# A decoder layer's projections: recorded in ticks, with products chained in PSUM, instead of placed by a scheduler

## The chip, the cores and the metric

The kernel runs on one core of one Trainium2 chip. The time is the device time of the whole program in microseconds (us), as the median of three runs. The profile is one further execution of the same program. The engines are named as the profile names them: PE is the matmul engine (PEld its weight loads), DVE the vector engine, ACT the scalar engine, POOL the GpSimd engine, SP the queue from which this kernel issues its DMAs. PSUM is the accumulator memory that PE writes and that ACT and DVE read, in banks of 512 fp32 columns; SBUF is the working memory.

## The reference

One layer of a hybrid decoder on 2048 tokens of width 1024, all in fp32:

```python
nx = rmsnorm(h, attn_norm_g[l])
proj = jnp.einsum('bsd,dp->bsp', nx, w_in[l])          # 1024 -> 3088 columns
gq, gk, gv, gr, glow, dq, dk_, dv_ = jnp.split(proj, split_at, axis=-1)
gate_pre = einsum(glow, gla_gate_w2[l]) + gla_gate_b[l]
glog = jax.nn.log_sigmoid(gate_pre) / GLA_TAU
o_a = gla_mixer(gq, gk, gv, glog)                       # gated linear attention, 4 heads
o_a = rms(o_a) * gla_norm_g[l] * jax.nn.silu(gr)
o_b = dilated_mixer(dq, dk_, dv_, rel_bias)             # windowed attention, 8 heads, 3 dilations
h = h + concat([o_a, o_b]) @ w_out[l]
h = h + square(relu(rmsnorm(h) @ w_ff1)) @ w_ff2
return rmsnorm(h, final_norm_g)
```

The change is in the first lines: the norm, the projection `proj`, the gate and the silu of `gr`. It also moves the factor `gla_norm_g` into the weights `w_out`.

## The kernel before

The program is one function, `emit`, and runs in stages: projections, the two mixers, the output projection, the MLP. An fp32 matmul is made of three fp32r matmuls (`mm3`, lines 136 to 138): a number is split into a high part (ACT copies it to fp32r, "hi") and a low part (DVE subtracts the high part, "lo"), and high by high, low by high and high by low are added up in PSUM.

The projection of 1024 inputs to 3088 columns is done in column groups: `dv` (256 columns twice), `gr` (264 twice, which hold the output gate and the 16 low-rank gate inputs), `gv` (256 twice), called wide here, and `dq`, `dk` (two groups each), `gq` and `gk` (128 twice), called narrow. Each group is computed for 1024 tokens (two blocks of 512) by the Strassen-Winograd scheme: the weights of a group and the tokens are cut into 2 by 2 blocks, and seven products `j` of their sums stand for eight. The token sums, split in hi and lo, stay in SBUF (`TF`, `TB`, tiles `tb`), one pair for each `j`; the second 1024 tokens are normed while the first are multiplied, kept in DRAM (`nTD`), and reloaded (`reload`). The sums of the weight blocks are made on POOL by `prep` (lines 278 to 284, tile `wraw`), which also splits them into `wcomb` (272 to 276).

A narrow product is 12 matmuls of 512 columns into one bank. A wide product is four times (once for each tile of 128 tokens) 12 matmuls of 256 or 264 columns. Each product has a bank of its own, and `product` takes it out at once: `rest` (lines 372 to 389) adds it to the blocks `CX`, `c11` to `c22` in SBUF (tile `acc`). Lines 372, 377 and 385 copy on ACT; 374, 379, 382 and 387 add a bank to a block on DVE; 380, 388 and 389 add block to block on DVE. `finish` then splits or gates the block and stores it; for `gr` it calls, for one tile of 128 tokens at a time, `log_sigmoid`, the multiplications 330 (DVE) and 331 (POOL) and `gate`.

The opening (the first eight token tiles: load, norm, eight transposes on PE, hi and lo) and the first products stand in an order written by hand (`manual_schedule`). From product 5 on the scheduler sets the order of every engine by its own estimate of time. The column groups go `dv, gr, dq, dk, dq, dk, gq, gk, gv`, twice.

The mixers follow. Their head tiles `qs`, `k`, `v`, `nb` are loaded while the last groups are multiplied.

Of the kernel before, what the change touches and what calls it, by code (L numbers as in the profile page):

```python
# [32 lines left out]
XG = (6, 7)  # L33
XSC = {0: (3,), 1: (4,), 2: (5,), 3: (), 4: (6,)}
TOP = (5,)
OTHER = [7, 9, 10, 11, 12, 13] + [14 * k + n for k in (1, 2, 3) for n in (0, 6, 9, 10, 11, 12)]
# [74 lines left out]
def emit(tc, a, stop=99):  # L111
# [37 lines left out]
    V.memset(mhalf, -0.5)  # L149
    xt = const.tile([128, 1024], F32, name="xt")  # L150
# [72 lines left out]
    misc = slot("misc")  # L223
    gB, gnB, w2b = misc[:, :D], misc[:, D:D + 512], misc[:17, D + 512:D + 768]
    gTs = [misc[:17, D + 768 + 128 * i:D + 896 + 128 * i] for i in range(2)]
    GP = 1056
    xp, bp, acc = slot("xp"), slot("bp"), [slot("acc") for _ in range(3)]
    CX, c11, c12, c21, c22, last = [t[:, GP * q:GP * q + GP] for t in acc for q in range(2)]
    C = [[c11, c12], [c21, c22]]
    stg_ring = view(last, (4, 264))  # L230
    xs = [t[:, D * q:D * q + D] for t in (xp, bp) for q in range(2)] + [c21[:, :D], last[:, :D]] * 2
    stg_at = [0]

    def stage():
        stg_at[0] = (stg_at[0] + 1) % 4
        return stg_ring[:, stg_at[0]]

    groups = [("dv", DV, 256), ("gr", GR, 264), ("dq", DQ, 128), ("dk", DK, 128), ("dq", DQ + 256, 128),
              ("dk", DK + 256, 128), ("gq", GQ, 128), ("gk", GK, 128), ("gv", GV, 256)]
    NG = len(groups)  # L240
    scales = {"dq": -0.125, "gq": 0.125}
    order = (1, 2, 5, 6, 3, 4, 7)
    jobs = [(g, j) for g in range(2 * NG) for j in order]
    w_in = a["w_in"].rearrange("o (c p) n -> p (o c) n", p=128)
    raws = [view(slot("wraw"), (2, 4, 264)) for _ in range(2)]
    combs = [slot("wcomb", FR) for _ in range(3)]
    TF = {j: [slot(f"tb{j}", FR) for _ in range(2)] for j in order}
    TB = {j: [view(t, (4, 512)) for t in TF[j]] for j in order}
    nTD = dram.tile([7, 128, 4, 512], F32, name="nTD")

    def load_w(g, n, k):

        if g < 2 * NG:
            _, c0, w = groups[g % NG]
            SP.dma_start(raws[n][:, k, :, :w], w_in[:, 4 * k:4 * k + 4, c0 + n * w:c0 + n * w + w])

    def comb(at, w):

        t = view(combs[at % 3], (2, 4, max(w, 256)))
        return [t[:, q, :, :w] for q in range(2)]  # L260

    def prep(at):

        if at >= len(jobs):
            return
        g, j = jobs[at]
        kind, _, w = groups[g % NG]
        (a11, a12), (a21, a22) = [[raws[n][:, k, :, :w] for k in range(2)] for n in range(2)]
        hi, lo = comb(at, w)
        src = {1: a11, 2: a12, 5: a21, 6: a21, 3: a12, 4: a22, 7: a21}[j]  # L270
        sc = scales.get(kind, 1.0)
        A.activation(hi, src, AF.Copy, scale=sc)  # L272
        if sc == 1.0:
            V.tensor_tensor(lo, src, hi.bitcast(F32), op=OP.subtract)  # L274
        else:
            V.scalar_tensor_tensor(lo, src, sc, hi.bitcast(F32), op0=OP.mult, op1=OP.subtract)
        if j == 2:
            G.tensor_tensor(a21, a21, a22, op=OP.add)  # L278
        if j == 5:
            G.tensor_tensor(a21, a21, a11, op=OP.subtract)  # L280
            load_w(g + 1, 0, 0)
            G.tensor_tensor(a12, a12, a21, op=OP.subtract)
        if j == 6:
            G.tensor_tensor(a21, a22, a21, op=OP.subtract)
        if j == 3:
            load_w(g + 1, 0, 1)
        if j == 4:
            load_w(g + 1, 1, 1)
        if j == 7:
            load_w(g + 1, 1, 0)  # L290

    def gate(glow, t):

        gT = gTs[t % 2]
        V.memset(gT, 1.0)
        pt = ps("d")
        T.transpose(pt[:16, :128], glow, ident)
        V.tensor_copy(gT[:16], pt[:16, :128])
        pg = ps("d")[:, :256]
        T.matmul(pg, gT, w2b, start=True, stop=True)  # L300
        e = stage()[:, :256]
        log_sigmoid(e, pg)
        SP.dma_start(glD[t * 128:t * 128 + 128], e)

    def finish(g, n, k, i):

        kind, c0, w = groups[g % NG]
        tb = 2 * (g // NG) + k
        c = C[n][k]
        if w == 128:  # L310
            tk = slice(512 * tb, 512 * tb + 512)
            if kind in ("gq", "gk"):
                SP.dma_start((gqD if kind == "gq" else gkD)[n, :, tk], c[:, :512])
                return
            pr = (c0 - (DQ if kind == "dq" else DK)) // 128 + n
            hi = c[:, 512:1024].bitcast(FR)
            A.activation(hi, c[:, :512], AF.Copy)
            V.tensor_tensor(c[:, :512], c[:, :512], hi.bitcast(F32), op=OP.subtract)
            SP.dma_start((qD if kind == "dq" else kD)[pr][:, :, tk], view(c, (2, 512)))
            return  # L320
        t = 4 * tb + i
        tk = slice(t * 128, t * 128 + 128)
        s = c[:, i * w:i * w + w]
        if kind == "gr":
            j = n * w
            m = min(w, 512 - j)
            sg = stage()[:, :m]
            log_sigmoid(sg, s[:, :m])
            A.activation(sg, sg, AF.Exp)
            V.tensor_tensor(s[:, :m], sg, s[:, :m], op=OP.mult)  # L330
            G.tensor_tensor(s[:, :m], s[:, :m], gnB[:, j:j + m], op=OP.mult)
            SP.dma_start(srD[tk, j:j + m], s[:, :m])
            if m < w:
                gate(s[:, m:w], t)
            return
        j = n * w
        if kind == "dv":
            SP.dma_start(token_rows(vN[:, j:], t, 512, w), s)
        if i == 3:
            SP.dma_start((vD if kind == "dv" else gvD)[512 * tb:512 * tb + 512, j:j + w].rearrange("(i p) n -> p i n", i=4),  # L340
                         c[:, :4 * w].rearrange("p (i n) -> p i n", i=4))

    banks = [0]

    def product(at, i):

        g, j = jobs[at]
        kind, _, w = groups[g % NG]
        p = ps("acao"[banks[0] % 4])
        banks[0] += 1  # L350
        B, W = TB[j], comb(at, w)
        n = w
        if w == 128:
            n = 512
            for c in range(4):
                mm3(p, W[0][:, c], W[1][:, c], B[0][:, c], B[1][:, c], c == 0, c == 3)
        else:
            p = p[:, :w]
            tk = slice(i * 128, i * 128 + 128)
            for c in range(4):  # L360
                mm3(p, B[0][:, c, tk], B[1][:, c, tk], W[0][:, c], W[1][:, c], c == 0, c == 3)
# [62 lines left out]
    def x_src(t):  # L424
        return (*xs[:6], c22[:, :D], c12[:, :D])[t]
# [1183 lines left out]
```

## Time and profile before

| | us |
|---|---|
| median of three runs | 2332.18 (2328.66 to 2334.69) |
| the profiled execution | 2329.67 |
| its span | 2327.9 |
| last matmul of the projections starts | 568.48 |
| first matmul of the mixers starts | 568.60 |

The span runs from the first to the last instruction. The profile's page gives the busy time of each engine; a matmul's record there runs until its result is written, so records of matmuls that follow each other overlap, and the busy time of PE says little about how densely they are issued. That is read from the distance between starts. A group's row reads: line, engine, operation, out<-in, out and in shape, count, then busy time, mean of one in ns, and the engine's idle time before it with what ended it. A stretch's row gives, for each engine, busy us and in brackets the number of instructions, then the granted clock of PE (1.00 is full), the DMA share and GB/s.

### The profile page before, as it was taken

The numbers are of one execution on the slowest core, as the hardware profiler recorded it, in microseconds if no ns is written. First come the engines' busy times: TensorE is split into PE (matmuls) and PEld (weight loads), VectorE is DVE, ScalarE is ACT, GpSimd is POOL, SyncE is SP. The second block draws the span as 40 slices with busy tenths as digits, with TensorE's granted clock in tenths as the row PEclk, the third lists the DMA queues.
The fourth block names the chain that finished last, engine by engine and source line by source line (L and its number), as shares of the span: only waits on it lengthen the run. The fifth ranks groups of instructions, "written<-read, shape, count | busy, mean of one in ns | idle before, by whom it ended". The sixth has DMA issues, their size and how long they took to land.

```text
span 2327.9 us, 35479 instructions
## 1 busy us (share of the span) xinstructions
PE 2256.6 (97%) x12456; PEld 1946.6 (84%) x12456; DVE 1698.2 (73%) x2925; ACT 1192.7 (51%) x2259; POOL 952.6 (41%) x879
## 2 busy tenths in 40 slices
PE   6999999999999997999999998999999999999998
PEld 5977889779999997888888886888888888888886
DVE  6889767866767777345677778877776968858997
ACT  5575435533777775223555556555563433333544
POOL 4343223434566779100023234323244535423665
PEclk9999999999999999999999999999999999999999
DMA  6457753767568675467644447444469564454573
GB/s 159 122 165 234 234 163 105 238 197 229 190 201 252 233 236 189 155 206 251 225 135 143 144 149 224 147 148 142 153 215 305 203 208 152 136 163 141 167 235 109
DMA packets 340369, 430.77 MB, mean 185 GB/s; under 512 B 20772, under 2 KB 270133, under 8 KB 333662
## 3 DMA queue, kind: packets, MB, share of 16 engines
q1 hardware_dynamic: 340046, 428.24, 57.9%
q8 instruction: 98, 1.61, 0.3%
q14 instruction: 81, 0.66, 0.1%
q10 hardware_dynamic: 144, 0.26, 0.0%
HBM read 276.60 MB, written 156.54 MB: 186 GB/s over the span
## 4 chain that ended last, share of the span: by engine, by line
PE 75%; DVE 9%; DMA 7%; issue 4%; ACT 2%; POOL 2%; SPq 0%; POOLq 0%; DVEq 0%; ACTq 0%
PE ps_a L136 9%; PE ps_a L138 9%; PE ps_a L137 9%; PE ps_c L137 6%; PE ps_c L138 6%; PE ps_c L136 6%; PE ps_a L754 4%; PE ps_d L136 3%; PE ps_d L138 3%; PE ps_d L137 3%; PE ps_d L735 3%; PE ps_c L713 2%; PE ps_c L715 2%; PE ps_o L136 2%; PE ps_o L137 2%
## 5 line engine op out<-in xcount | busy, mean ns | idle before, releaser
L1163 ACT ACTIVATE w1comb<-w1raw 128x512 fp32r<-128x512 f32 x224 | 141.4, 632 | 238.9 <-PE ps_a L138 81.8
L1342 ACT ACTIVATE cs<-rs 128x1024 fp32r<-128x1024 f32 x104 | 109.6, 1055 | 225.7 <-PE ps_c L138 137.6
L1168 DVE TENSOR_TENSOR w1comb<-w1raw,w1comb 128x512 fp32r<-128x512 f32 x224 | 176.1, 787 | 27.7 <-ACT w1comb L1163 27.7
L726 ACT ACTIVATE pe<-pe,O 128x256 f32<-128x256 f32 (+1 forms) x384 | 155.9, 454 | 56.7 <-DVE O L725 52.0
L754 PE MATMUL ps_a<-v,pt 128*128 128x65 f32 x1200 | 178.7, 250 | 0.7 <-DVE pt L744 0.7
L754 PEld LDWEIGHTS ps_a<-v,pt 128*128 128x128 f32 x1200 | 174.5, 193 | 2.3 <-DVE pt L744 0.9
L735 PE MATMUL ps_d<-ident,pe 128*128 128x128 f32 x600 | 159.1, 278 | 0.0
L725 DVE CUSTOM_DVE_ANT_0 pe<-ps_c,nb 128x256 f32<-128x256 f32 (+1 forms) x384 | 126.8, 361 | 42.6 <-PE ps_d L735 17.4
L136 PE MATMUL ps_a<-hb,w1comb 128*128 128x512 f32 x384 | 149.6, 390 | 1.8 <-ACT xt L1211 1.8
L137 PE MATMUL ps_a<-hb,w1comb 128*128 128x512 f32 x384 | 149.5, 389 | 0.4 <-DVE w1comb L1168 0.4
L138 PE MATMUL ps_a<-hb,w1comb 128*128 128x512 f32 x384 | 149.4, 389 | 0.0
L164 POOL TENSOR_TENSOR stats<-stats,mhalf 128x1 f32<-128x1 f32 (+1 forms) x64 | 48.8, 764 | 245.6 <-DVE stats L163 245.6
L1384 DVE TENSOR_TENSOR ct<-rt,ct 128x1024 fp32r<-128x1024 f32 x68 | 137.1, 2016 | 14.6 <-ACT ct L1380 14.5
L272 ACT ACTIVATE wcomb<-wraw 128x512 fp32r<-128x512 f32 (+2 forms) x126 | 96.7, 773 | 94.8 <-POOL wraw L278 19.6
L137 PE MATMUL ps_c<-ct,cs 128*128 128x512 f32 x360 | 140.1, 389 | 0.0
L136 PE MATMUL ps_c<-ct,cs 128*128 128x512 f32 x360 | 140.1, 389 | 0.0
L138 PE MATMUL ps_c<-ct,cs 128*128 128x512 f32 x360 | 140.1, 389 | 0.0
L1268 POOL TENSOR_TENSOR acc<-acc 128x256 f32<-128x256 f32 x75 | 69.8, 941 | 160.8 <-DVE acc L1268 149.7
L274 DVE TENSOR_TENSOR wcomb<-wraw,wcomb 128x512 fp32r<-128x512 f32 (+2 forms) x84 | 101.4, 1212 | 38.4 <-ACT wcomb L272 34.6
L1268 POOL TENSOR_TENSOR xt<-acc,acc 128x256 f32<-128x256 f32 x32 | 28.2, 883 | 229.8 <-ACT acc L1230 214.1
L1349 DVE SCALAR_TENSOR_TENSOR cs<-rs,cs 128x1024 fp32r<-128x1024 f32 (+1 forms) x56 | 96.8, 1736 | 30.1 <-ACT cs L1342 29.9
L136 PE MATMUL ps_a<-wcomb,tb 128*128 128x256 f32 (+1 forms) x336 | 98.6, 294 | 10.7 <-ACT acc L385 3.4
(353 smaller groups left out, 7661.8 us busy)
## 6 DMA issues: line engine op xcount, KB each, us to landing
rs<-actD SPq DMA_DIRECT2D x103, 512.0 KB, 4.3
actD<-acc SPq DMA_DIRECT2D x288, 128.0 KB, 2.8
w1raw<-w_ff SPq DMA_DIRECT2D x32, 1024.0 KB, 6.3
rt<-w_ff SPq DMA_DIRECT2D x24, 1024.0 KB, 7.6
k<-kD SPq DMA_DIRECT2D x16, 1024.0 KB, 8.3
rb<-hTD SPq DMA_DIRECT2D x13, 1024.0 KB, 6.4
wraw<-w_in SPq DMA_DIRECT2D x48, 256.0 KB, 3.7
cmb<-boD SPq DMA_DIRECT2D x16, 528.0 KB, 5.9
```

The costliest lines, as they stand in the source:

```text
L136: T.matmul(out, sh, mh, start=first, stop=False, skip_group_check=more)
L137: T.matmul(out, sl, mh, start=False, stop=False, skip_group_check=more)
L138: T.matmul(out, sh, ml, start=False, stop=last, skip_group_check=more)
L274: V.tensor_tensor(lo, src, hi.bitcast(F32), op=OP.subtract)
L725: V.tensor_tensor_reduce(p, s, bias, scale=1.0, scalar=BIG, op0=OP.add, op1=OP.min, accum_out=nm)
L726: A.activation(p, p, AF.Exp, bias=nm, scale=-1.0)
L735: T.transpose(pb[:, i * 128:i * 128 + 128], src, ident)
L754: T.matmul(self.b.opsum[:, n % 4], self.pt[:, i * 128:i * 128 + 128], self.b.v[:, blk, cols], start=first, stop=last)
L1163: A.activation(c[:, 0], v, AF.Copy)
L1168: V.tensor_tensor(c[:, 1], v, c[:, 0].bitcast(F32), op=OP.subtract)
L1342: A.activation(v[:, 0], x, AF.Copy, scale=float(PRODUCTS[ph // 2][2]))
L1384: V.tensor_tensor(v[:, 1], x, v[:, 0].bitcast(F32), op=OP.subtract)
```

## The change

The stage of the projections is written again. All five engines run it in program order, and the order comes from a list of ticks: `on(t, f, ...)` enters a step, and the loop plays the ticks and records, after a tick's other steps, that tick's matmuls. One tick is 12 matmuls of a wide product (one token tile) or half a narrow product; a wide group is 28 ticks, a narrow one 14. The hi of a product stands five to seven ticks ahead of it, the lo three or four, the evictions one to three behind.

- Products are chained in PSUM. `rest` formed Winograd's sums by adding blocks. Now bank U takes P1, then P6, then P7, and bank W takes P5, then P3, by matmuls that go on adding into the same bank (`more`), and the bank is copied out in between. A group's products go 1, 2, 6, 5, 7, 4, 3. Two tiles of a wide product share one bank. Only `gr` keeps a bank for each product and tile.
- The weight sums are others (four, of which two in each narrow group of the first half are on POOL; all the rest on DVE).
- `dv` of the first 1024 tokens is computed plainly, tile by tile, 24 matmuls of 512 columns each (`dv_piece`), while the tiles are loaded, normed and transposed. So the first Strassen group is `gr`, at tick 32, and there are 17 groups.
- `gr` is gated by whole blocks of four tiles (`gated`, `gate`); `gla_norm_g` is multiplied into `w_out` instead.
- The gain row of the first norm is loaded once and spread over the partitions by two matmuls; 14 transposes of the identity precede it.

The core of the diff:

```diff
-            if j == 1:
-                A.activation(ix, q, AF.Copy)
-            elif j == 2:
-                V.tensor_tensor(i11, q, ix, op=OP.add)
-                finish(g, 0, 0, i)
-            elif j == 5:
-                A.activation(i22, q, AF.Copy)
-            elif j == 6:
-                V.tensor_tensor(ix, q, ix, op=OP.add)
-                V.tensor_tensor(c12, X, c22, op=OP.add)
-            elif j == 3:
-                V.tensor_tensor(i12, q, i12, op=OP.add)
...
-                V.tensor_tensor(ix, q, ix, op=OP.add)
-                V.tensor_tensor(c21, c21, X, op=OP.add)
-                V.tensor_tensor(c22, c22, X, op=OP.add)
...
+        name = {1: "U", 6: "U", 7: "U", 5: "W", 3: "W"}.get(j, "Y") if kind != "gr" else "Y"
+        more = kind != "gr" and j in (6, 7, 3)
+        if w == 128:
+            if i == 0 and not more:
+                held[name, g % 2] = bank()
+            p = held[name, g % 2]
+            for c in (2 * i, 2 * i + 1):
+                mm3(p, W[0][:, c], W[1][:, c], B[0][:, c], B[1][:, c], c == 0 and not more, c == 3, more)
...
+        if j == 1:
+            A.activation(d11, U, AF.Copy)
+        elif j == 6:
+            A.activation(d12, U, AF.Copy)
+        elif j == 7 and not part:
+            A.activation(d21, U, AF.Copy)
+        elif j == 7:
+            V.tensor_tensor(d22, W, d21, op=OP.add)
+        elif j != 5:
+            to, p = {2: (d11, Y), 4: (d21, Y), 3: (d12, W)}[j]
+            V.tensor_tensor(to, p, to, op=OP.add)
...
+            h, l = (b - 5, b - 3) if L == 2 or (early and x == 0) else (b - 7, b - 4)
...
+                on(b + 2, evict, at, 0)
+                if j == 7:
+                    on(b + 3, evict, at, 0, 1)
+        if L == 2:
+            Ps = G if g < 7 else V
+            for n, t, X in ((0, -4, Ps), (1, -2, V), (2, 0, Ps), (3, 2, V)):
+                on(B + t, wsum, g, n, X)
+            for n, k, t in ((0, 0, 5), (1, 1, 12), (1, 0, 13), (0, 1, 15)):
+                for step, dt in enumerate((0, 1, 2)):
+                    on(B + t + dt, finish_narrow, g, n, k, step)
...
+            if n < 8:
+                on(4 * t + 1, tile_T, n)
+                on(4 * t + 2, tile_hi, n)
+                on(4 * t + 2, tile_lo, n)
+                on(4 * t + 3, tile_keep, n)
+                on(4 * t + 4, sums_G, n)
...
+            for m in range(4):
+                on(4 * t + m, dv_piece, t, m)
```

Where it moves instructions, at three places. The opening on PE, up to the second tile's first matmuls. Before (L449 are transposes, L136 to L138 the product 1 of `dv` for tile 0):

```order
L449 MATMUL ps_c<-ident,xp 128x128 x4
L449 MATMUL ps_d<-ident,xp 128x128 x4
L136 MATMUL ps_a<-wcomb,tb_119 128x256
L137 MATMUL ps_a<-wcomb,tb_120 128x256
L138 MATMUL ps_a<-wcomb,tb_119 128x256
```

And now (L724 the identity, L727 the gain row, L649 transposes, L132 to L134 the plain `dv`):

```order
L724 MATMUL ps_a<-ident 128x128 x14
L727 MATMUL ps_c<-xt,one 128x512
L727 MATMUL ps_d<-xt,one 128x512
L649 MATMUL ps_c<-ident,xp 128x128 x4
L649 MATMUL ps_a<-ident,xp 128x128 x4
L132 MATMUL ps_d<-tb_126,tb_114 128x512
L133 MATMUL ps_d<-tb_126,tb_115 128x512
L134 MATMUL ps_d<-tb_127,tb_114 128x512
```

The first products now take all the columns of `dv` at once, with the token tile as the stationary operand.

DVE in the back half of a narrow `dq` group, before: evictions (380 to 389), the splits of the weights (274) and of a finished block (318), the second half's token sums (503 to 508):

```order
L380 TENSOR_TENSOR acc<-acc 128x512
L382 TENSOR_TENSOR acc<-ps_a,acc 128x4x16x8
L503 TENSOR_TENSOR xp<-bp 128x512
L274 TENSOR_TENSOR wcomb<-wraw,wcomb 128x4x128
L507 TENSOR_TENSOR xp<-bp,xp 128x512
L508 TENSOR_TENSOR xp<-xp,bp 128x512
L318 TENSOR_TENSOR acc<-acc 128x512
L274 TENSOR_TENSOR wcomb<-wraw,wcomb 128x4x128
L387 TENSOR_TENSOR acc<-ps_a,acc 128x4x16x8
L274 TENSOR_TENSOR wcomb<-wraw,wcomb 128x4x128
L388 TENSOR_TENSOR acc<-acc 128x512
L389 TENSOR_TENSOR acc<-acc 128x512
```

And now, in a `dq` group of the second half (360 and 363 read a bank, 379 splits a finished block, 288 the weights, 295 are weight sums of the next group, 445 is the gate):

```order
L295 TENSOR_TENSOR wraw<-wraw 128x4x128
L360 TENSOR_TENSOR acc<-ps_a,acc 128x4x16x8
L288 TENSOR_TENSOR wcomb<-wraw,wcomb 128x4x128
L363 TENSOR_TENSOR acc<-ps_o,acc 128x4x16x8
L295 TENSOR_TENSOR wraw<-wraw 128x4x128
L379 TENSOR_TENSOR acc<-acc 128x512
L288 TENSOR_TENSOR wcomb<-wraw,wcomb 128x4x128
L445 SCALAR_TENSOR_TENSOR xt<-ps_d,xt 128x512 x2
L363 TENSOR_TENSOR acc<-ps_a,acc 128x4x16x8
```

Of the five evictions here three are left, each out of a bank; in the whole group seven became four. The weight sums came to DVE.

POOL in the narrow groups of the first half, before (278 to 284 are the four weight sums, 331 the gating of `gr`, 164 a norm's root):

```order
L331 TENSOR_TENSOR acc<-acc,misc 128x248 x4
L278 TENSOR_TENSOR wraw<-wraw 128x4x128
L331 TENSOR_TENSOR acc<-acc,misc 128x248
L280 TENSOR_TENSOR wraw<-wraw 128x4x128
L282 TENSOR_TENSOR wraw<-wraw 128x4x128
L284 TENSOR_TENSOR wraw<-wraw 128x4x128
```

And now (163 is the root, and after the last row of these POOL has no weight sums any more):

```order
L295 TENSOR_TENSOR wraw<-wraw 128x4x128 x6
L163 TENSOR_TENSOR stats<-stats,mhalf 128x1 x2
L295 TENSOR_TENSOR wraw<-wraw 128x4x128 x2
L163 TENSOR_TENSOR stats<-stats,mhalf 128x1 x2
L295 TENSOR_TENSOR wraw<-wraw 128x4x128 x2
```

POOL now makes 12 of the 68 weight sums, where it made all 72, and none of the 32 multiplications of line 331.

757 lines of the change are left out of this document (471 added, 286 removed).

## The prediction, made before the changed kernel ran

> **What bounds the kernel now.** First the page: engines, then the span in slices.
>
> ```profile
> PE 2256.6 (97%) x12456; PEld 1946.6 (84%) x12456; DVE 1698.2 (73%) x2925; ACT 1192.7 (51%) x2259; POOL 952.6 (41%) x879
> PE   6999999999999997999999998999999999999998
> DVE  6889767866767777345677778877776968858997
> PEclk9999999999999999999999999999999999999999
> ```
>
> PE is the bound throughout; the change can only remove time in which PE issues nothing. The projections are the first ten slices, with DVE nearly as full as PE. So next the stretches: the opening, the other projections, the mixers, the rest.
>
> ```profile
> 0.00:100.00 100.00, 76.33 (x520) 71.72 (x520) 69.18 (x96) 49.31 (x86) 45.08 (x32) 0.95 0.56 148
> 100.00:568.60 468.60, 452.19 (x2687) 392.81 (x2688) 348.99 (x526) 230.79 (x457) 166.06 (x124) 0.99 0.62 188
> 568.60:933.00 364.40, 350.98 (x3095) 343.28 (x3094) 265.82 (x1054) 253.94 (x709) 255.76 (x369) 0.99 0.68 221
> ```
>
> Of these, the same view of the products alone (tile wcomb), then of the transposes (tile ident):
>
> ```profile
> 0.00:100.00 100.00, 67.12 (x456) 62.53 (x456) 16.82 (x11) 11.49 (x11) 0.95 0.56 148
> 100.00:568.60 468.60, 434.82 (x2568) 380.21 (x2568) 117.94 (x115) 85.16 (x115) 0.99 0.62 188
> ```
>
> ```profile
> 0.00:100.00 100.00, 11.43 (x64) 9.63 (x64) 0.50 (x2) 0.95 0.56 148
> 100.00:568.60 468.60, 13.69 (x80) 8.73 (x80) 0.00 (x0) 0.99 0.62 188
> ```
>
> How long does a product's matmul hold PE? Records overlap, so I take the distance of starts in two dense stretches: in the chain, 37 steps of 512 columns; in the timeline, 43 steps of 256.
>
> ```profile
> 519.83 0.23 PE ps_a L137
> ...
> 528.22 0.23 PE ps_o L138
> ```
>
> ```profile
> 563.32 0.28 PE L137 MATMUL ps_a<-wcomb,tb 128*128 128x256 f32 x1
> ...
> 568.48 0.28 PE L138 MATMUL ps_o<-wcomb,tb 128*128 128x256 f32 x1
> ```
>
> 8.39 / 37 = 0.227 us and 5.16 / 43 = 0.120 us; for 264 columns I scale to 0.124. The groups by line and shape give the counts (three lines each, so three times these):
>
> ```profile
> L136 PE MATMUL ps_a<-tb,wcomb 128*128 128x512 f32 x168 | 66.3, 395 | 0.0
> L136 PE MATMUL ps_c<-tb,wcomb 128*128 128x512 f32 x84 | 34.3, 409 | 1.8 <-ACT wcomb L272 1.8
> L136 PE MATMUL ps_o<-tb,wcomb 128*128 128x512 f32 x84 | 33.2, 395 | 1.3 <-ACT acc L377 1.3
> L136 PE MATMUL ps_a<-wcomb,tb 128*128 128x264 f32 x112 | 32.0, 286 | 1.2 <-DVE acc L374 1.2
> L136 PE MATMUL ps_c<-wcomb,tb 128*128 128x264 f32 x56 | 16.0, 285 | 0.0
> L136 PE MATMUL ps_o<-wcomb,tb 128*128 128x264 f32 x56 | 16.1, 287 | 1.7 <-DVE acc L374 1.7
> L300 PE MATMUL ps_d<-misc 17*128 17x256 f32 x32 | 11.1, 426 | 0.0
> ```
>
> Opening: 456 x 0.120 = 54.7 us of products and 11.4 of transposes in 100 us; 33.9 lost. After 100 us: 1008 x 0.227 = 228.8, 672 x 0.124 = 83.3, the other 2568 - 1680 = 888 x 0.120 = 106.6, transposes 13.7, gate 11.1: 443.5 of 468.6; 25.1 lost. Together 59 us. (Busy time overstates transposes and gate, so the loss is rather more; a few us of it are bias rows and first scores.)
>
> **The opening.** Its durations, and its chain's first links:
>
> ```profile
> 5.43 1.06 ACT L429 ACTIVATE tb<-xp 128x1024 fp32r<-128x1024 f32 x1 [3.44 <-DMA xp<-x]
> 8.25 1.11 PE L449 MATMUL ps_c<-ident,xp 128*128 128x128 f32 x4 [8.25 <-DVE xp L441]
> L416 ACT ACTIVATE tb<-ps_d 128x512 fp32r<-128x512 f32 x8 | 4.7, 586 | 0.0
> L272 ACT ACTIVATE wcomb<-wraw 128x1024 fp32r<-128x1024 f32 x28 | 29.4, 1054 | 31.5 <-PE ps_c L137 5.9 <-PE ps_o L137 5.4 <-PE ps_o L138 5.0
> L495 DVE SCALAR_TENSOR_TENSOR xp<-xp,stats,misc 128x1024 f32<-128x1024 f32 x8 | 10.2, 1280 | 4.7 <-POOL stats L164 4.4
> L417 DVE TENSOR_TENSOR tb<-ps_d,tb x8: 675/678/681, 12.8 to 68.2; 128x512 fp32r<-128x512 f32 x8
> L417 DVE TENSOR_TENSOR tb<-acc,tb x8: 681/1610/1781, 43.5 to 66.6; 128x512 fp32r<-128x512 f32 x8
> 30.00:40.00 10.00, 7.27 (x41) 7.07 (x41) 8.71 (x10) 6.62 (x13) 8.13 (x5) 0.72 0.20 56
> ```
>
> Tile 0 is transposed at about 8.7 us, its first plain matmul comes at 11.7; nothing is won there. Then ACT's order decides: for each of tiles 1 to 3 a square (1.06 and a read of 0.19), a weight split (1.05), two copies hi and two to keep (4 x 0.59), each behind the transposes that wait for DVE's scale (1.28) and PE's piece. Walked through, tile 1 is transposed at 18, tile 2 at 28, tile 3 at 34, and the pieces of tiles 0 to 2 are done at about 39 us. PE has then done 3 x 24 x 0.227 = 16.3 and 4 x 1.43 (11.43 / 8) = 5.7: 17 lost. For tiles 3 to 7 PE has 24 x 0.227 + 1.43 = 6.9 us each. DVE has four reads of PSUM (0.68), the scale, a root (0.15) and two splits of SBUF tiles (0.68 alone, 1.61 beside POOL): 5.5 to 7.4. So up to 0.5 a tile is lost, 2 us; and 3 for the slow clock seen in the row 30 to 40 (0.72), which a broken-up opening will meet again. Loss 22 us; the ends are 16 (no clock loss, DVE within PE) and 30 (near the 33.9 of before, which has the same chain with less ACT work).
>
> The Trainium skill, "SBUF — State Buffer", § "SBUF: two separate sides", says that DVE and POOL share a port pair as an exclusive lock, so that a DVE operation with two SBUF inputs waits out a whole POOL operation that reads SBUF. The rows of L417 agree (0.68 out of PSUM, up to 1.78 between SBUF tiles). By that rule both POOL sums of a tile could hold DVE up in full and a tile would take 8 to 9 us, the loss 28; by the median row it is 22.
>
> **Added PE work.** `dv` of the first half: 8 x 24 x 0.227 = 43.6 instead of 7 x 4 x 12 x 0.120 = 40.3, so +3.3. The identity and gain matmuls lie ahead of 8.7 us, where PE has nothing else: nothing. The gates' and all other matmuls are the same in number.
>
> **From tick 32 on.** A narrow group is 84 x 0.227 = 19.1 us of PE, a wide one 336 x 0.120 = 40.3 (`gr` 41.7). Against that:
>
> ```profile
> L274 DVE TENSOR_TENSOR wcomb<-wraw,wcomb 128x1024 fp32r<-128x1024 f32 x28 | 44.3, 1583 | 17.3 <-ACT wcomb L272 13.7 <-DMA wraw<-w_in 3.6
> L276 DVE SCALAR_TENSOR_TENSOR wcomb<-wraw,wcomb 128x512 fp32r<-128x512 f32 x42 | 33.3, 799 | 14.0 <-ACT wcomb L272 13.9
> L318 DVE TENSOR_TENSOR acc<-acc 128x512 f32<-128x512 f32 x32 | 31.2, 989 | 0.7 <-ACT acc L317 0.5
> L374 DVE TENSOR_TENSOR acc<-ps_c,acc 128x512 f32<-128x512 f32 x3 | 2.7, 910 | 0.0
> L374 DVE TENSOR_TENSOR acc<-ps_a,acc 128x264 f32<-128x264 f32 x4 | 1.7, 426 | 1.3 <-PE ps_a L138 1.1 <-issue 0.2
> L330 DVE TENSOR_TENSOR acc<-acc 128x264 f32<-128x264 f32 x16 | 12.1, 756 | 2.1 <-ACT acc L329 1.5
> ```
>
> DVE in a `dq` group at these (mixed) means: 7 splits x 0.80, 4 evictions x 0.91, 4 finishing splits x 0.99, 2 sums on DVE x 0.80 (4 in the second half): 14.8 to 16.4 of 19.1. Pairs of second-half tokens add 2 scales and four of 0.68, 5.6 us in 18 ticks, or 4.4 a group: 19.2, just PE's 19.1 plus its transposes, in the first half only, and there the means fall, because POOL's 72 sums and 32 multiplications shrink to 12 sums. `gr` has 28 evictions of 0.43 (row L374, 264 columns), 7 splits and 4 sums of about 1.3, two gatings of a whole block (8 x 0.76 a pair by row L330, less for four tiles at once: 2.6 each) and the gate's 2: 36 of 41.7, plus 8 leftover splits of the opening. DVE does not become the bound, but is near it at two places.
>
> The new waits: PE goes on in bank U only after ACT has copied it, two ticks (2.7 us) later, and in bank W one tick (1.36) after DVE has read it. Behind a late copy ACT's later splits queue, which are five ticks ahead. The copies into `c12` wait for the store of the group before:
>
> ```profile
>   DMA kD<-acc: 11.8, 4
>   DMA qD<-acc: 6.3, 4
> DMA to landing us min/median/max: 3.2/5.0/10.5
> ```
>
> (What ACT line 377 waits for; how long `qD`'s stores take.) The store of `c12` is issued three ticks into the next group (4.1 us), product 7 needs the copy at tick 8 (10.9) and the copy takes 0.6: a landing up to 6 us is free, the median 5.0 passes, the longest costs 4. I take 3 us for two such stores, 2 for W and 2 around `gr`: 7 us lost. The ends are 0 (all within the slack) and 25 (as before).
>
> The end: the last products leave two evictions instead of twelve; PE's first mixer work waits less, 1 us. What comes after has the same instructions; its order is the scheduler's again, at the handover to the output projection too, and I count it as 0, +/- 4.
>
> **Sum.** Against the execution of 2329.7 us: 59 lost before, 22 + 7 lost after, 3.3 added, 1 gained at the end: 59 - 29 - 3.3 + 1 = 28 us less, 2302. The median of the runs is 2.5 above that execution, so 2304.
>
> **Rivals.**
> - *Banks wait for stores (slower).* ACT's copy of U in product 6 waits for the landing of `c12`'s store, PE waits for ACT, eight times (four `dq`/`dk` groups in each half). It cancels the gain when each loses 28 / 8 = 3.5 us, at a mean landing of 9.5 us, and decides for slower at 10.5. For it: 10.5 was seen. Against: the median is 5.0. At 11 us: 2304 + 8 x 5 = 2344. Chance 0.07; a milder form, no change (2325 to 2339): 0.10.
> - *DVE becomes the bound.* W's reads have one tick; if DVE runs behind, each of 12 narrow groups loses about 1 us, the opening 28 instead of 22: 18 us of the gain go, 2304 + 13 to 18 = 2319. For it the 19.2 above. Chance 0.17 for 2312 to 2325.
> - *A cold PE.* All of the opening's first ten pieces (6 x 0.227 each) at half speed is 13.6 more, half of it inside waits: 2311. The Trainium skill, "TensorE: Matmul & The Clock Gate", § "HAM oscillation — how this bites in real kernels", warns of idle gaps over about 3.4 us; the row with 0.72 agrees. It is inside the range.
> - *Order holds better than I think.* Loss 16 and 0, and the loss before as large as starts alone make it: 40 to 45 us less, under 2290. Chance 0.11.
>
> **Numbers.** Likeliest, 0.55: 2290 to 2312. A measurement tells 0.3%, 7 us, from no change. Faster 0.83, same 0.10, slower 0.07. The range 2283 to 2324 takes the likeliest, most of the DVE case and the nearer half of the best one.
>
> **What would show it.** The first mixer matmul at about 540 instead of 568.6; tick 32 (the first `gr` matmul, now 264 columns) near 76 us; POOL under 60 us of busy time ahead of it; DVE's sums and splits near 0.68 and 1.22 in the second half. Wrong would be: PE idle before matmuls of U or W behind ACT or DVE evictions, ACT waiting for `qD`/`kD`, or an opening past 85 us.

## Result: 42 us faster, 14 more than forecast, of which the handover that was counted at nothing gave 11.5

| | before | changed |
|---|---|---|
| median of four runs, us | 2332.72 (2328.66 to 2334.69) | 2290.59 (2289.33 to 2293.59) |
| ratio of the times | | 0.9823 (95% interval 0.9806 to 0.984) |
| the profiled execution | 2329.67 | 2293.59 |
| its span | 2327.9 | 2291.8 |

The two profiled executions differ by 36.1 us; the other 6 are their places among the runs (the one before 3 below its median, the one after 3 above). Single traces below are to be read with that 3 us. In the later runs the kernel before had medians of 2329.1 to 2330.3; against these the changed kernel is 38 to 40 us faster.

The page of the changed kernel: engines, then PE and its clock in slices.

```profile
PE 2246.9 (98%) x12330; PEld 1935.6 (84%) x12330; DVE 1618.2 (71%) x2780; ACT 1162.8 (51%) x2088; POOL 804.0 (35%) x785
PE   8998999999999999999999998999999999999998
PEclk9999999999999999999999999999999999999999
```

PE is still the bound; DVE lost 80 us of work and POOL 149. Where the time went is read at four marks: the first `gr` matmul (264 columns), the first score of the mixers, the first matmul of the MLP, the end. First the changed kernel's marks in the timeline (start, us), then its stretches between them, then those of the kernel before.

```profile
71.23 0.28 PE L132 MATMUL ps_a<-wcomb,tb 128*128 128x264 f32 x1
545.78 0.30 PE L937 MATMUL ps_c<-k,qp 128*128 128x256 f32 x1
1093.46 0.48 PE L132 MATMUL ps_a<-hb,w1comb 128*128 128x512 f32 x1
```

```profile
0.00:71.20 71.20, 63.92 (x274) 48.86 (x275) 45.70 (x60) 36.34 (x62) 20.05 (x22) 1.00 0.61 171
71.20:545.78 474.58, 459.18 (x2810) 408.41 (x2808) 305.73 (x420) 215.98 (x310) 36.95 (x35) 0.99 0.59 190
545.78:1093.46 547.68, 541.96 (x4058) 504.65 (x4057) 353.68 (x1184) 307.83 (x807) 270.94 (x394) 1.00 0.68 221
1093.46:2291.80 1198.34, 1181.88 (x5195) 973.66 (x5193) 913.05 (x1118) 602.67 (x909) 476.01 (x334) 1.00 0.54 172
```

```profile
0.00:79.40 79.40, 56.03 (x355) 51.65 (x356) 55.73 (x78) 43.14 (x75) 35.31 (x28) 0.94 0.54 139
79.40:568.60 489.20, 472.49 (x2855) 412.89 (x2854) 362.44 (x544) 236.96 (x469) 175.83 (x127) 0.99 0.62 188
568.60:1127.79 559.19, 545.77 (x4060) 507.27 (x4059) 357.31 (x1188) 309.69 (x807) 270.09 (x392) 0.99 0.67 217
1127.79:2327.90 1200.11, 1182.28 (x5195) 974.76 (x5193) 922.76 (x1118) 602.95 (x909) 471.36 (x334) 1.00 0.53 172
```

The projections won 8.2 and 14.6, together 22.8 us (in the kernel before, 46 of `dv`'s 336 matmuls, 5.5 us, still came behind the first `gr` matmul, so the opening's true share is 13.7 and the rest's 9.1). The stretch from score to MLP won 11.5 with hardly an instruction changed, the MLP 1.8.

What is still lost in the projections, in the changed kernel's timeline (a value in brackets is PE's idle time and what ended it), chain and list of waits (total, times, longest):

```profile
188.77 0.39 PE L134 MATMUL ps_a<-tb,wcomb 128*128 128x512 f32 x1
192.92 0.50 PE L132 MATMUL ps_c<-tb,wcomb 128*128 128x512 f32 x1 [3.76 <-ACT acc L356]
219.41 0.50 PE L132 MATMUL ps_a<-tb,wcomb 128*128 128x512 f32 x1 [2.97 <-ACT acc L356]
```

```profile
183.81 0.62 DVE acc L363
184.44 7.75 DMA qD<-acc
...
192.27 0.61 ACT acc L356
```

```profile
ACT acc L356 <- DMA kD<-acc: 10.7, 2, 6.1
ACT bp L553 <- DMA xp<-x: 10.4, 6, 2.8
```

These are the forecast's wrong signs: PE stands before a matmul of bank U, ACT (line 356, the copy into `c12`) waits for `qD` and `kD`. But ACT also waits six times for tokens of the second half (line 553, the square). Which is the cause, and what the handover's 11.5 us are, the experiments had to tell.

### The profile page after: what moved, and what is told of

It reads as the page before. It is cut to its first block, busy times and chain, and to the rows that moved or that the text cites. A ratio compares the mean times of both kernels' runs of the same rounds, so it can differ in the third digit from the quotient of the medians.

```text
span 2291.8 us, 34438 instructions
## 1 busy us (share of the span) xinstructions
PE 2246.9 (98%) x12330; PEld 1935.6 (84%) x12330; DVE 1618.2 (71%) x2780; ACT 1162.8 (51%) x2088; POOL 804.0 (35%) x785
## 4 chain that ended last, share of the span: by engine, by line
PE 82%; DMA 6%; DVE 5%; issue 2%; POOL 2%; ACT 2%; SPq 0%; POOLq 0%; DVEq 0%; ACTq 0%
PE ps_a L134 9%; PE ps_a L132 9%; PE ps_a L133 9%; PE ps_c L132 8%; PE ps_c L133 7%; PE ps_c L134 7%; PE ps_a L978 4%; PE ps_d L134 3%; PE ps_d L132 3%; PE ps_d L133 3%; PE ps_d L959 3%; PE ps_c L937 2%; PE ps_c L939 2%; PE ps_o L132 2%; PE ps_o L134 2%
## 5 line engine op out<-in xcount | busy, mean ns | idle before, releaser
L891 POOL CAST qp<-qs 128x512 fp32r<-128x512 f32 x64 | 65.6, 1103 | 270.2 <-PE ps_c L133 252.5
L132 PE MATMUL ps_a<-hb,w1comb 128*128 128x512 f32 x384 | 150.1, 391 | 1.6 <-ACT xt L1450 1.6
L134 PE MATMUL ps_a<-hb,w1comb 128*128 128x512 f32 x384 | 150.2, 391 | 0.0
L1623 DVE TENSOR_TENSOR ct<-rt,ct 128x1024 fp32r<-128x1024 f32 x68 | 132.4, 1947 | 17.5 <-ACT ct L1619 17.5
L132 PE MATMUL ps_c<-ct,cs 128*128 128x512 f32 x360 | 140.1, 389 | 0.0
L134 PE MATMUL ps_c<-ct,cs 128*128 128x512 f32 x360 | 140.1, 389 | 0.0
L283 ACT ACTIVATE wcomb<-wraw 128x512 fp32r<-128x512 f32 (+2 forms) x119 | 89.1, 755 | 51.9 <-DVE wraw L295 28.0
L959 PEld LDWEIGHTS ps_d<-ident,pe 128*128 128x128 f32 x600 | 108.8, 186 | 0.2
```

The source lines that it names most:

```text
L132: T.matmul(out, sh, mh, start=first, stop=False, skip_group_check=more)
L134: T.matmul(out, sh, ml, start=False, stop=last, skip_group_check=more)
L959: T.transpose(pb[:, i * 128:i * 128 + 128], src, ident)
L1623: V.tensor_tensor(v[:, 1], x, v[:, 0].bitcast(F32), op=OP.subtract)
```

## Experiments

All times are medians; the kernel before, run beside them, stood at 2329.1 to 2330.3. "The stretch" is the time from the first matmul of the output projection to the first of the MLP: 216.8 us before (911.02 to 1127.79), 204.9 changed (888.57 to 1093.46).

**The handover: one part of the change alone.** In the kernel before:

```diff
-            G.tensor_tensor(s[:, :m], s[:, :m], gnB[:, j:j + m], op=OP.mult)
...
-            A.activation(w[:, 0], raw, AF.Copy)
+                A.activation(w[:, 0], raw, AF.Copy, scale=gn[:, c:c + 1])
```

> The kernel before with one part of the change alone: gla_norm_g is multiplied into w_out instead of into the gated block (32 POOL multiplications of 264 columns less). The changed kernel went from its first mixer score to its first MLP matmul in 547.7 us, the kernel before in 559.2: 11.5 us that the change has no instruction for but this one. My theory: those come from the order in which the scheduler happens to interleave POOL's merging of the last heads, not from where the gain is multiplied. Then this kernel lies within 5 us of the kernel before (2328 to 2338 us) in the projections, and its stretch from mixer score to MLP may lie anywhere from 546 to 562. Rival: moving the gain shortens the handover; then that stretch is 546 to 550 and the time 2319 to 2323 us.

2319.59 us, ratio 0.9949 (0.9929 to 0.9969): the rival's time, and yet not the rival. The stretch is 215.4; the first score comes at 561.2 instead of 568.6. So 7.4 of the 10 us lie in the projections, where 32.6 us of POOL multiplications are gone and the scheduler was free to place the rest anew; which of the two it was is not separated. My 0 to 5 us there was wrong, and so would have been a verdict by the time alone.

**The handover: less work ahead on POOL.** In the kernel before:

```diff
-                running[pr, t0] = combine(pr, t0, n, got[pr, t0 // 8], V if (pr, t0) == (3, 12) else G)
+                running[pr, t0] = combine(pr, t0, n, got[pr, t0 // 8], V if (pr, t0) in ((2, 8), (3, 12)) else G)
```

> The kernel before, with the merging of the second half of head pair 2 on DVE instead of POOL (10 POOL operations of about 1.0 to 1.3 us on blocks of 512, and the small ones stay). From the first matmul of the output projection to the first of the MLP the kernel before takes 216.8 us, all kernels in ticks 203.5 to 205.1, the kernel before with only the gain moved 215.4. My theory: POOL's queue decides that. It ends the first merged block of the last pair 352.7 us after the first score in the kernel before and 344.7 in the changed one, and PE has meanwhile nothing but 24 matmuls. Relieved here by 10 to 12 us of POOL work just ahead, the block is merged earlier and the stretch falls to 204 to 209, the time to 2319 to 2326 us, if DVE takes the work for nothing. Rival: DVE's own chain of small operations at the end decides; then the stretch stays at 214 to 218 and the time at 2328 us or more.

2327.96 us, ratio 1.0 (0.9983 to 1.0018), stretch 216.1: my theory of POOL's load fell. POOL even waited 1.45 us for DVE there, and then still did six multiplications (line 812, 911.2 to 917.5 us) ahead of the first addition (814). That points at the order. PE in the kernel before, POOL beside it, and POOL in the changed kernel (1036 is the multiplication, 1038 the addition):

```profile
919.79 0.39 PE L138 MATMUL ps_a<-wo,mT 128*128 128x512 f32 x1
924.21 0.48 PE L449 MATMUL ps_d<-ident,O 128*128 128x128 f32 x1 [4.04 <-POOL O L814]
930.10 0.90 PE L449 MATMUL ps_d<-ident,mx 128*128 128x128 f32 x3 [5.41 <-DVE mT L417]
```

```profile
912.25 1.05 POOL L812 TENSOR_TENSOR O<-O,small 128x512 f32<-128x512 f32 x1
913.25 2.04 POOL L812 TENSOR_TENSOR cmb<-cmb,small 128x512 f32<-128x512 f32 x2
915.25 1.04 POOL L812 TENSOR_TENSOR O<-O,small 128x512 f32<-128x512 f32 x1
916.25 2.05 POOL L812 TENSOR_TENSOR cmb<-cmb,small 128x512 f32<-128x512 f32 x2
918.26 1.29 POOL L814 TENSOR_TENSOR O<-O,cmb 128x512 f32<-128x512 f32 x1
921.30 1.29 POOL L814 TENSOR_TENSOR O<-O,cmb 128x512 f32<-128x512 f32 x1
```

```profile
885.41 1.04 POOL L1036 TENSOR_TENSOR O<-O,small 128x512 f32<-128x512 f32 x1
886.41 2.04 POOL L1036 TENSOR_TENSOR cmb<-cmb,small 128x512 f32<-128x512 f32 x2
888.74 1.28 POOL L1038 TENSOR_TENSOR O<-O,cmb 128x512 f32<-128x512 f32 x1
890.46 1.28 POOL L1038 TENSOR_TENSOR O<-O,cmb 128x512 f32<-128x512 f32 x1
```

Before, two blocks are multiplied together and PE waits for the first one's additions; in the changed kernel each block is finished before the next.

**The handover: POOL's order alone.** In the kernel before, from the last six units of the mixers on:

```diff
+        if k == NU - 6:
+            pin.enter_context(tc.manual_schedule(engines={nc.gpsimd.engine}))
```

> The kernel before with POOL's instructions in program order from the last six units of the mixers on; every instruction is the same. So far the scheduler placed the six multiplications of two merged blocks of the last head pair ahead of the first block's two additions; in program order each block's three multiplications are followed by its two additions, as they stand in the changed kernel. My theory, after the kernel with less POOL work ahead did not shorten the stretch (216.1 us): not POOL's load but this order makes PE wait at the output projection, 4.2 and 5.8 us with the clock at half behind it. Then the stretch from the first matmul of the output projection to the first of the MLP falls from 216.8 to 203 to 208 us and the time by 8 to 12, 2318 to 2322 us. Rival: DVE's chain of small operations ends last whatever POOL does; the stretch stays at 214 to 218 and the time at 2326 us or more.

2318.36 us, ratio 0.9956 (0.9941 to 0.9971), no wait over 1.8 us left at the handover. Its marks, by the timeline:

```profile
914.53 0.48 PE L136 MATMUL ps_a<-wo,mT 128*128 128x512 f32 x1
1120.99 0.47 PE L136 MATMUL ps_a<-hb,w1comb 128*128 128x512 f32 x1
```

The stretch is 206.5: 10.3 of the 11.9 us by which the changed kernel shortens it, with every instruction as before. (In this trace the mixers ahead were 4.1 us longer, so 6.2 net; the medians say 10.7.) The clock, granted 0.66 over 920 to 940 us in the kernel before, is 1.00 over the same stretch here, so the gain is the waits and the slow clock behind them. So POOL's order at the end of the mixers alone gives 6.2 (trace) to 10.7 us (medians), and the changed kernel has that order. All ten kernels in ticks, the changed one among them, have a stretch of 203.3 to 205.1. Why the scheduler orders the tail otherwise behind the new projections stays open.

**Is it chaining?** The changed kernel, with a bank for every product and the block sums as before:

```diff
-        name = {1: "U", 6: "U", 7: "U", 5: "W", 3: "W"}.get(j, "Y") if kind != "gr" else "Y"
-        more = kind != "gr" and j in (6, 7, 3)
+        name, more = "Y", False
```

> The changed kernel with every product in a bank of its own again, taken out by itself and added block to block in SBUF as before the change; ticks and program order stay. My theory: the order carries the gain and chaining only relieves DVE. By the means of the trace a narrow group then has three more DVE additions (2 reads of PSUM at about 0.8 us and one of 0.68), 2.3 us on top of the 15 to 16.5 of 19.1 us, and 4.4 of scales and sums beside it in the first half: DVE lies about 2 us over PE in four or five groups. The projections end 8 to 15 us later than the 545.8 us of the changed kernel, the time is 2299 to 2306 us. Rival: chaining carries the gain; then the 23 us that the projections won go, the first mixer score comes at 565 us or later and the time is 2313 or more. Other rival: evictions are hidden altogether, 2288 to 2294.

2295.16 us (2294.85 to 2296.54), 4.6 more than the changed kernel, first score at 548.4. Chaining is worth 5 of the 42 us. The rest of the projections' gain lies in what this kernel still shares with the changed one: ticks and program order, the plain `dv`, the gating by whole blocks, the gain moved into `w_out` and the sums moved to DVE. Moving the gain alone gave 7.4 us there in the kernel before. The new steps in the scheduler's order were not run, so the share of the order by itself is not shown. DVE has 341 us instead of 306 between 71 and 545 us and still isn't the bound. And bank U is not there any more, but PE waits at nearly the same place:

```profile
195.41 0.90 PE L551 MATMUL ps_d<-ident,xp 128*128 128x128 f32 x3 [5.11 <-DVE xp L568]
229.39 0.87 PE L551 MATMUL ps_d<-ident,xp 128*128 128x128 f32 x3 [4.90 <-DVE xp L568]
```

**Is it the store?** The store of `c12` two ticks later, and, the other way, a second buffer for it:

```diff
-                for step, dt in enumerate((0, 1, 2)):
+                for step, dt in enumerate((0, 1, 4 if (n, k) == (0, 1) else 2)):
```

> The changed kernel with the store of the last block (c12) of each narrow group issued two ticks (2.7 us) later, and nothing else. My theory: the three waits for ACT's copy of bank U into c12 in the trace (3.9, 3.1 and 0.7 us) are landings of that store. Then each of these grows by 2.7 us, and of the other five crossings of dq and dk those with a landing over 3.5 us lose what is over: 8 + about 6 = 10 to 18 us more, 2301 to 2309 us, with PE idle ahead of product 7 in most groups. Rival: the waits come from the loads of x queued ahead on ACT and the store has slack; 0 to 4 us more, at most 2295.

2297.33 us (2294.49 to 2299.17): 6.7 more, less than my 10 and more than the rival's 4. One wait grew from 2.97 to 7.89 us, the others stayed: the store is near the limit at one crossing, not at eight.

```diff
+    def block_of(g, n, k):
+        return last if (n, k) == (0, 1) and g % 9 in (2, 4, 6) else C[n, k]
...
-        c = C[n, k]
+        c = block_of(g, n, k)
```

> The changed kernel with the block c12 of every second narrow group in another buffer (last), so that ACT's copy of bank U never waits for the store of the group before. Nothing else differs. My theory: the x cycle is what is late, so PE's wait only moves from the copy into c12 to the transposes of x, as in the unchained kernel, where the copies were gone and PE waited 5.3, 5.1 and 2.5 us for the scaled x: 0 to 4 us less, 2287 to 2291 us. Rival: the store's landing (7.75 us for one) is the limit; then 7 us or more go, 2283 us or less, and no wait of over 1 us stands at 160 to 230 us.

2290.99 us (2288.56 to 2293.93): nothing. With the copy free, the wait moved to the addition behind it:

```profile
223.58 0.79 PE L132 MATMUL ps_c<-tb,wcomb 128*128 128x512 f32 x1 [4.70 <-DVE acc L363]
```

**Is it the cycle of the x loads?** Pairs of second-half tokens every 20 ticks, with the stores out of the x buffer ahead of the others and the reloads moved to fit:

```diff
-            for j, v in (((2, b21), (1, b11), (5, b12)), ((6, t2), (3, b22)), ((4, t4), (7, t3)))[step - 14]:
+            for j, v in (((6, t2), (4, t4), (7, t3)), ((2, b21), (1, b11)), ((5, b12), (3, b22)))[step - 14]:
...
-            on(base[0] + 51 + 18 * i + dt, pair, i, step)
+            on(base[0] + 51 + 20 * i + dt, pair, i, step)
...
-        t = base[7] + 10 + 21 * n // 4
+        t = base[7] + 16 + 18 * n // 4
```

> The changed kernel with the second half's token pairs started every 20 ticks instead of 18, the three stores out of the x buffer put ahead of the four out of the other, and the reloads moved back by 6 ticks at a spacing of 4.5. My theory: PE's waits between 160 and 260 us in the changed kernel (3.9, 3.1, 2.6, 1.2, 1.1 us) all come from one cycle that is longer than its 18 ticks (24.5 us): load of x, 6.8 us to landing, 9 ticks of squares to differences, stores issued 0.7 to 0.9 us apart and 3.75 to landing, then the next load; ACT waited 10.4 us for x there, and its copies of bank U queued behind. With the cycle fitted these waits go: 8 to 12 us less than the changed kernel, 2279 to 2283 us, first mixer score at 534 to 538. Rival: the waits are those of c12's own store; then this gives 0 to 3 us, 2288 to 2291.

2281.16 us (2280.01 to 2284.53), 9.4 less, first score at 530.3. The work is the same, only begun less often and stored in another order. ACT's waits for x, in the changed kernel six of 10.4 us, are in this kernel:

```profile
  ACT bp L553: 6.0, 3
```

So most of the loss from 160 to 260 us went with this edit. Counted by the matmuls of the products, number 529 starts at 150.07 us in the changed kernel and at 148.34 here, number 951 at 262.09 and 250.21: 10.2 us are won between them. (The traces are 15.5 us apart at the first score, but 1.7 of it is the opening and 2.4 the clock at the bias products, told below.) The reading: a load of 6.8 us, nine ticks of work (12.2), three issues of 0.7 to 0.9 us and a store of 3.75 add up to about 25 us, in 18 ticks (24.5 us). ACT, in program order, stood before the late square, and all behind it, the copy of U too, was late. Period, order of the stores and reloads were changed together, so which of them did it is not separated. One wait of 2.56 us remains, up to 190.1 us.

**Sums on POOL or DVE.** All weight sums of the narrow groups on POOL; and the token sums of the opening on DVE:

```diff
-            for n, t, X in ((0, -4, Ps), (1, -2, V), (2, 0, Ps), (3, 2, V)):
+            for n, t, X in ((0, -4, G), (1, -2, G), (2, 0, G), (3, 2, G)):
```

> The changed kernel with all four weight sums of every narrow group on POOL (48 instead of 12); nothing else differs. My theory: POOL's sums run beside DVE's splits and slow those between SBUF tiles (in the trace before, 0.68 us alone and up to 1.78 beside POOL), and each sum comes about 1 us later, but DVE loses 36 additions of 0.68 us; PE loses 0 to 6 us more than now, 2291 to 2297 us. Rival: taking the sums off POOL was what won time in the narrow groups; then each of 12 groups loses 1 us or more again and the time is 2303 or more. Other rival: DVE is the limit there, and freed of 24 us the projections end earlier, 2283 to 2288.

2288.9 us (2286.45 to 2291.12), the runs overlap with the changed kernel's (2289.33 to 2293.59): no difference that these runs can tell. That POOL is rid of the narrow groups' sums is not what won.

```diff
-        G.tensor_tensor(b21, b21, t2, op=OP.subtract)
-        G.tensor_tensor(b11, t2, b11, op=OP.subtract)
+        V.tensor_tensor(b21, b21, t2, op=OP.subtract)
+        V.tensor_tensor(b11, t2, b11, op=OP.subtract)
```

> The changed kernel with the 8 token sums of the opening on DVE instead of POOL. In the changed kernel these take POOL 15.1 us (1.5 to 2.2 each) and DVE's 8 splits beside them take 1.48 us on average instead of 0.68. My theory: DVE gains 8 x 0.8 = 6.4 us and pays 8 x 0.68 = 5.4, and PE's opening loses little there (4 us between 30 and 71): 0 to 2 us either way, 2289 to 2293 us, the splits at about 0.70. Rival, the opening bound by the port that DVE and POOL share: with POOL gone the first matmul of gr comes 3 us or more earlier, 2287 us or less.

2290.31 us, first `gr` matmul at 70.3: nothing, as expected. The eight splits between SBUF tiles in the opening, by form, in the changed kernel and in this one:

```profile
L687 DVE TENSOR_TENSOR tb<-acc,tb 128x512 fp32r<-128x512 f32 x8 | 11.5, 1480 | 2.2 <-ACT tb L683 2.2
L687 DVE TENSOR_TENSOR tb<-acc,tb 128x512 fp32r<-128x512 f32 x8 | 5.2, 688 | 0.4 <-ACT tb L683 0.4
```

A split takes 0.8 us longer beside POOL's sums. The Trainium skill ("SBUF — State Buffer", § "SBUF: two separate sides") says that DVE and POOL hold a shared port pair by turns, as an exclusive lock; the rows agree. But PE is not waiting for the splits.

**The clock.** Without the 14 transposes of the identity; and the bias products in three ticks:

```diff
-        for _ in range(14):
-            T.transpose(warm[:, :128], ident, ident)
```

> The changed kernel without the 14 transposes of the identity at the start. My theory, as predicted: they lie where PE has nothing else to do (1.3 to 4.2 us, the first transposes of x at 10.6) and cost nothing; without them the gain's matmuls and the first pieces still find the clock granted, and the time is 2289 to 2292 us, the first matmul of gr within 1 us of 71.2. Rival, the cold PE: without them PE runs slow for the first pieces, as the kernel before did between 30 and 40 us (granted clock 0.72): 3 to 7 us more, 2294 to 2298.

2290.03 us: nothing. The first `gr` matmul comes at 70.0; in the eight kernels with the transposes and the same opening it comes at 69.4 to 71.7. The same stretch, first in the changed kernel, then in this one:

```profile
15.00:20.00 5.00, 4.28 (x11) 2.47 (x10) 2.42 (x2) 1.13 (x2) 0.03 (x1) 1.00 1.05 248
15.00:20.00 5.00, 4.38 (x15) 3.07 (x13) 1.35 (x2) 1.02 (x2) 0.00 (x0) 0.66 1.05 256
```

By the clock's column (1.00 and 0.66) the transposes seem to keep the clock up. The starts say otherwise. Two steps of 512 columns of the first pieces, in the changed kernel and in this one:

```profile
14.12 0.63 PE L132 MATMUL ps_d<-tb,tb 128*128 128x512 f32 x1
14.55 0.63 PE L133 MATMUL ps_d<-tb,tb 128*128 128x512 f32 x1
```

```profile
12.47 0.40 PE L132 MATMUL ps_d<-tb,tb 128*128 128x512 f32 x1
12.71 0.40 PE L133 MATMUL ps_d<-tb,tb 128*128 128x512 f32 x1
```

They start 0.43 us apart with the transposes and 0.24 without. The changed kernel's trace holds no record of the clock before 20.0 us, and the column shows 1.00 where there is none; up to there PE ran at half speed, the 14 transposes too (0.21 us apart, against 0.108 later). In two other traces with the same opening (three bias ticks, pairs every 20) the records begin at 4.3 and 4.6 us, and the column is 0.50 from 7.7 to 17.9 and from 8.0 to 18.2. So the transposes did not keep the clock up for the first pieces, and they put off the gain's matmuls by 2.1 us (4.52 instead of 2.46).

```diff
-    on(base[9] + 60, bias_rows)
+    for d, dt in ((-1, 60), (0, 61), (1, 62), (2, 63)):
+        on(base[9] + dt, bias_rows, d)
```

> The changed kernel with the three bias products in three ticks instead of all in one, the sign change a tick ahead. In the changed kernel PE waits 1.4 us there, does six matmuls of 33 rows by 8 in 2.8 us, and then 14 matmuls at a granted clock of 0.50 to 0.60 (200 ns more each). My theory: broken up among products the clock stays up and the wait goes: 3 to 5 us less, 2286 to 2288 us. Rival: the clock falls for another reason at that place and 0 to 1 us is won.

2289.32 us (2287.1 to 2293.54): in the trace PE's loss between 420 and 440 us falls from 4.3 to 0.4 us, but the runs overlap, so the gain is not shown by the time. Nor is the cause: in three other kernels with all six together the clock did not fall (last section). The stretch, changed kernel and this one:

```profile
431.00:434.00 3.00, 3.00 (x8) 2.29 (x8) 2.35 (x4) 0.00 (x0) 0.00 (x0) 0.50 0.43 117
427.00:430.00 3.00, 3.00 (x13) 1.60 (x11) 1.73 (x3) 1.47 (x2) 0.00 (x0) 1.00 0.40 155
```

**Together**: pairs every 20 ticks, sums on POOL, bias in three ticks, `c12` in two buffers.

> The changed kernel with four edits at once: pairs every 20 ticks with their stores and reloads moved, all weight sums of narrow groups on POOL, the bias products in three ticks, c12 in two buffers. From the single runs: pairs 9.4 us less than the changed kernel, sums on POOL 1.7, bias 1.3, c12 nothing. If they add up, 2276 to 2280 us; where sums and c12 were hidden behind the late loads of x they may show now, 2272 at best. Rival: POOL's sums beside DVE's splits, and the pairs' later end beside the reloads, cost what they win; then it is no better than 2281.

2276.26 us (2274.5 to 2278.88), ratio to the kernel before 0.9772 (0.9749 to 0.9796), first score at 527.5: better than both kernels, 14 us less than the changed one.

## Why the prediction was right, and where its terms were not

The direction and the range held, and PE does stand less, with the work in a fixed order; that the order is the reason is shown only in part (the unchained kernel). The time missed by 13 us. By its own steps, with the losses now taken from starts throughout (four transposes are 0.43 us apart, gate matmuls 0.216):

| term | forecast | measured |
|---|---|---|
| lost before, opening | 33.9 | 100 - 54.7 - 7.0 = 38.3 |
| lost before, after 100 us | 25.1 | 468.6 - 228.8 - 83.3 - 106.6 - 8.7 - 7.0 = 34.2 |
| lost in the new opening | 22 (16 to 30) | 71.2 - 43.6 - 7.0 = 20.6 |
| lost from tick 32 on | 7 (0 to 25) | 474.6 - 228.8 - 83.3 - 121.0 - 8.7 - 7.0 = 25.8 |
| plain `dv` | 3.3 | 3.3, not measured apart |
| after the projections | 0, +/- 4 | 11.5 + 1.8 = 13.3 |

Projections: 38.3 + 34.2 - 20.6 - 25.8 - 3.3 = 22.8, the measured 568.60 - 545.78, against 28 (27.7) forecast.

- *The opening* came out as walked through: first plain matmul at 12.4 (11.7 forecast), the pieces of tiles 0 to 2 issued by 39.4 (39). Tick 32 came at 71.2 instead of 76, mostly because the transposes take 7.0 us by starts and not the 11.4 of their busy time. The 3 us for a slow clock were met, and the 14 transposes did not spare them: up to 20.0 us PE ran at half speed, though the column shows 1.00. An estimate from the starts: twelve matmuls of 512 columns at 0.43 instead of 0.227 us and twelve transposes at about 0.22 instead of 0.108 make 3.8 us, part of it inside waits.
- *The loss before* was 13.5 us larger, for the reason the text gives in brackets: records of transposes and gate overlap.
- *Tick 32 on* is the step that failed: 25.8 us, just past its upper end. I looked for waits at the banks and at `c12`'s store and found the right places, but not their cause. I counted each step of a token pair by its engine, and never summed the cycle through both transfers against its 18 ticks. The run with 20 ticks showed 9.4 us of it (10.2 in the traces).
- *What comes after* was put at 0, +/- 4: the other step that failed. The stretch behind the projections, whose order the text leaves to the scheduler, gave 11.5 us; POOL's order there, set by itself in the kernel before, gave 6.2 to 10.7.
- *Signs*: first score 545.8 instead of 540; POOL 20.05 + 36.95 = 57.0 us ahead of it (under 60); DVE's sums and splits in the second half as forecast:

```profile
L295 DVE TENSOR_TENSOR wraw<-wraw 128x512 f32<-128x512 f32 x24 | 16.4, 683 | 0.1
L288 DVE TENSOR_TENSOR wcomb<-wraw,wcomb 128x1024 fp32r<-128x1024 f32 x15 | 18.6, 1248 | 4.5 <-ACT wcomb L283 4.5
```

- *Rivals.* Banks that wait for stores: seen at a few crossings, far from eight. DVE as the bound: no, 35 us more of it cost 4.6. A cold PE in the opening: in part, two pieces of the ten at half speed, which the forecast had in its 3 us. Order that holds better: the time is at its edge (2290), but not by its way; the loss is 20.6 and 25.8, not 16 and 0.

One side sum is off: the terms that the forecast lists for DVE in `gr` add up to 33.5 us, not 36. Nothing else hangs on it.

The 42 us are thus 22.8 + 11.5 + 1.8 in the traces and 6 between traces and medians. That 28 came near the 22.8 of the projections was luck: the loss before was 13.5 us larger than forecast and the loss left 17.4 larger (46.4 instead of 29), and the two nearly cancel.

## What to carry to other kernels

For work with a period, add up the whole cycle, transfers and issue times included, and hold it against the period before looking at any single wait: an engine in program order turns one late load into waits at places that have nothing to do with it. When a stage is rewritten, the scheduler may order the next ones anew, here with 11.5 us, half of what the rewritten stage won; read those stages' order too, and pin it where a few operations stand before the bound engine. A kernel that lands on a forecast time has not shown the forecast's reason: look where in the trace the time went. And hold a clock column of 1.00 against the distance of starts: it also stands where the trace has no record of the clock.

## What the runs showed of the hardware

PE's clock (the column of the stretches behind POOL's) fell behind the wait of 3.76 us in the changed kernel, and not behind the one of 2.97:

```profile
192.00:198.00 6.00, 5.08 (x19) 4.33 (x20) 3.61 (x3) 1.64 (x3) 1.93 (x1) 0.72 0.23 63
219.40:223.00 3.60, 3.58 (x16) 2.98 (x17) 0.84 (x2) 2.15 (x4) 0.30 (x1) 1.00 0.97 248
```

Behind the waits of 4.70 to 7.89 us in three other kernels it was 0.50 to 0.54 over the next 4 us. The Trainium skill ("TensorE: Matmul & The Clock Gate", § "HAM oscillation — how this bites in real kernels") puts the limit at idle gaps of about 3.4 us. These rows agree, but others of this case do not. In the kernel with all narrow sums on POOL the clock fell behind a wait of 2.93 us at the same place (0.65 over the next 4 us), and in the kernel before, in the row of 0.72 that the forecast shows, behind waits of 1.98 and 2.73 us. So a shorter wait can cost the clock too; what decides it is not found here. Not expected: it also fell to 0.50 where PE had stood only 1.23 us and then issued six matmuls of 33 rows by 8, in 2.9 us:

```profile
426.70 0.39 PE L134 MATMUL ps_o<-tb,wcomb 128*128 128x512 f32 x1
428.31 2.89 PE L520 MATMUL ps_d<-xp 33*8 33x384 f32 x6 [1.23 <-DVE xp L517]
431.13 0.79 PE L132 MATMUL ps_a<-tb,wcomb 128*128 128x512 f32 x1
```

Of the eight kernels that issue the same six together behind a wait of 1.23 us, five show this. In the three others (pairs every 20 ticks, narrow sums on POOL, two `c12` buffers) the clock was 1.00 over the 10 us from the first of them, as it was where they stand two at a time among products. Whether such small matmuls count as idle for the clock was not tried by itself.
